# A two-layer hybrid transformer in one fp32 kernel: work from VectorE to ScalarE, and attention on two-bank PSUM tiles

## The chip, the core and the metric

The kernel runs on one core of a Trainium2 chip, in one launch. The metric is the device time in microseconds (us), the median of the runs. The engines that appear are TensorE (PE; its weight loads are PEld), VectorE (DVE), ScalarE (ACT), GpSimd (POOL) and SyncE (SP, which issues the loads of weights).

## The reference

Two layers over a sequence of 256 tokens (the latents) and a context of 256 tokens, width 1024. Each layer is a SwiGLU FFN, a mixer and another FFN, each behind an RMS norm that is scaled and shifted by a modulation, and added back through a gate. The first layer's mixer is a gated depthwise convolution, the second's is attention with 8 query heads and 2 key heads of 128. The second layer's context stream ends after it has given keys and values, and its second FFN runs on the latents alone.

```python
def _modulate(t, g, shift, scale):
    return _rms(t, g) * (1 + scale) + shift

def _swiglu(h, w13, w2):
    gte, up = jnp.split(h @ w13, 2, axis=-1)
    return (jax.nn.silu(gte) * up) @ w2

def _attend(q, k, v):
    s = jnp.einsum('bqhgd,bkhd->bhgqk', q, k).astype(jnp.float32) * (ATTN_HEAD_DIM ** -0.5)
    p = jax.nn.softmax(s, axis=-1).astype(v.dtype)
    return jnp.einsum('bhgqk,bkhd->bqhgd', p, v)
...
        mod = (jax.nn.silu(c) @ mod_w[i] + mod_b[i]).reshape(bsz, 3, 3, 1, D_MODEL)
        modc = (jax.nn.silu(c_ctx) @ mod_w[i] + mod_b[i]).reshape(3, 3, D_MODEL)
        lat = lat + 0.5 * mod[:, 0, 2] * _swiglu(_modulate(lat, norm_g[i, 0], mod[:, 0, 0], mod[:, 0, 1]), ffn_w13[i, 0], ffn_w2[i, 0])
...
        if kind == MIX_CONV:
            y = _short_conv_mixer(h, conv_w_in[j], conv_k[j], conv_w_out[j])
...
        elif kind == MIX_ATTN:
            y, yc = _gqa_mixer(h, hc, ctx_out, attn_w_qkv[j], attn_q_g[j], attn_k_g[j], attn_w_o[j], cos, sin)
...
        lat = lat + mod[:, 1, 2] * y
```

## The kernel before

Activations lie with the features on the 128 partitions and the tokens along the free axis: `x` holds 8 feature tiles (`KT`) of 512 tokens (`T2`), 256 (`S`) of the latents (stream 0) and 256 of the context (stream 1). Every fp32 operand of a product is split into a high part rounded for TensorE (`fp32r`) and the remainder: `split` gives ScalarE the copy into the high part (L98, tiles `wh`, `gh`, `pth`) and VectorE the subtraction for the low one (L99, `wl`, `gl`, `ptl`). A product is then three matmuls, high by high, high by low and low by high (`mm3`, L122 to L124). Weights come in raw tiles `wr` of 128x2048, three buffers, loaded by SyncE, and are split in halves of 1024.

**FFN.** The 22 hidden tiles of an FFN are done in thirds of 8, 7 and 7 (`THIRDS`); behind each third `project` multiplies by w2 and `finish` adds the gated result to `x` (L446, VectorE, one step for each stream). Most hidden tiles of the first three FFNs are pairs (class `Pair`): gate and up of one hidden tile are a 2x2 block product done with seven products of half depth in place of eight (a scheme of Strassen's kind, with sums of weights `S1` to `S4`, sums of activations `T1` to `T4`, and the blocks `A11`, `A12`, `A22`). There are 54 pairs. A pair has two PSUM tiles: `p` gathers A11, S2, S3 and A22 in turn, its middle results read off by ScalarE, and `q` holds A12 in its first half and S1 and S4 in its second. `head` does A11 into p, copies it to `sg` (L585) and does A12 into q; `five` does S1 and copies it to `gm` (L591); `six` does S2, copies p to `sg` (L595), does S4, adds (L597) and applies Silu (L598); `seven` does S3 and adds (L602); `four` does A22 and multiplies (L608). The loop puts `seven` and `four` of the pair before between `five` and the end of `six` of the next pair. `sums` builds the sums of weights (L557, L563, L567) in a tile `ws`. The first pair of a third has no pair before it.

**Modulation.** The modulations of both layers are products of a row with a matrix. VectorE does them, one unit of 1024 columns for one feature tile and one stream at a time (`mod_unit`, L142, multiply and sum; its elementwise output goes to `junk`). `tick` gives out these units as filling work along the kernel: each stage calls it with a number of units that are then due, and loads the next raw tile when needed.

**Norms.** `square_add` squares on ScalarE and adds up on VectorE, one addition for each stream; `rms_inv` gets the inverse root; `norm_k` and `Blocks.block` scale on VectorE and ScalarE, and `block` also makes the T sums.

**Attention.** For each of 8 heads `scores` makes, for each half of 128 queries, a score tile of one bank `psc` (512 keys), its maximum (L1042), the bias `nb` (L1044), the exponential with its sum (L1050), 1/sum `r` (L1054), and the normalized `pn` on GpSimd (L1058). `turn` transposes pn on TensorE (L1067) into `pt`, two tiles of one bank, and splits them; `mix` multiplies with the values into `pav` and splits the result. All PSUM tiles come from one pool of six banks, and a second of two small ones. The loop runs:

```python
    for hd in range(HEADS):
        if hd + 2 < HEADS:
            pns[hd + 2] = scores(hd + 2)
        pts[hd] = turn(pns.pop(hd))
        if hd:
            mix(hd - 1, pts.pop(hd - 1))
        tick(2)
```

**Last FFN.** It runs on the latents alone. Its first 4 hidden tiles use the input before its norm (`first_mm`, a 256-token product with two more columns that carry the shift; the norm is applied behind it, `first_post`), while the norm is worked out; all eight normalized blocks are made behind tile 1. The others use `mm2`, where the high and low part lie side by side in one moving tile of 512 (L1107, L1108).

The program is written as one order of work; a scheduler then places each engine's instructions, so that an engine's order may differ from the written one. Engines wait for each other on semaphores. A tile from a pool waits until the last reader of the buffer that it takes is done.

## Time and profile before

| | us |
|---|---|
| median of 3 runs | 1587.94 |
| lowest, highest | 1587.75, 1588.68 |
| the profiled execution | 1589.78 |
| span of its trace (first to last instruction) | 1588.0 |
| mean granted clock of TensorE | 0.995 |

The profiled execution takes 1.8 us more than its span, and lies 0.1% over the median. In the page's rows an engine's busy time comes with its share of the span and the number of its instructions. In a row of a group stand the line, the engine, the operation, the tiles it writes and reads, and its count; then busy time, mean ns of one, and the idle time of the engine just before, with what ended it. Matmuls are pipelined: a record of 0.28 us overlaps the next, and the step from start to start is the price of one. The wait rows give the total, the number and the longest of the waits of a line.

### The profile page before, as it was taken

The page shows a single profiled execution, that of the slowest core. Times are in us where ns is not written, and L with a number is a line of the kernel's source. Part 1 is how long each engine was busy: PE and PEld are TensorE (multiplying, and loading weights), DVE is VectorE, ACT ScalarE, POOL GpSimd, SP SyncE. Part 2 cuts the span into 40 slices and gives each one's busy share as a digit, 9 for nine tenths or more (in the row PEclk, how much of TensorE's full clock was granted, in tenths as well). Part 3 has the DMA queues.
Part 4 walks back from the last instruction along what each step waited for, and adds up shares of the span by engine and source line. Part 5 has one row for each costly group of instructions (what it writes and reads, how often), then busy time and mean ns, then how long its engine had stood idle before and what let it go on. Part 6 is the DMA issues. An engine that isn't in the chain of part 4 may idle for free.

```text
span 1588.0 us, 25040 instructions
## 1 busy us (share of the span) xinstructions
PE 1565.0 (99%) x10210; PEld 1423.9 (90%) x10210; DVE 1319.8 (83%) x2029; ACT 738.2 (46%) x1180; POOL 29.8 (2%) x20
## 2 busy tenths in 40 slices
PE   8999999999999999999999999999999999899998
PEld 6788998998888899989899899899899898888887
DVE  5778778879998879799798899898898899976654
ACT  5532452544322356335345375335255455655543
POOL 0000000000000000000000000000000005200000
PEclk9999999999999999999999999999999999999999
DMA  8545234234565412452342423443433654645552
GB/s 319 181 174 201 92 115 167 104 117 162 186 214 193 177 65 95 142 200 104 130 177 102 160 103 107 158 161 107 175 133 122 235 186 149 234 156 186 186 202 90
DMA packets 38419, 248.74 MB, mean 157 GB/s; under 512 B 5280, under 2 KB 7072, under 8 KB 11936
## 3 DMA queue, kind: packets, MB, share of 16 engines
q1 hardware_dynamic: 35712, 245.38, 43.5%
q10 hardware_dynamic: 2592, 1.76, 0.4%
q8 instruction: 80, 1.31, 0.3%
q14 instruction: 35, 0.29, 0.1%
HBM read 244.77 MB, written 1.05 MB: 155 GB/s over the span
## 4 chain that ended last, share of the span: by engine, by line
PE 93%; DVE 3%; ACT 2%; DMA 1%; issue 1%; POOL 0%; DVEq 0%; POOLq 0%; ACTq 0%
PE py L122 9%; PE py L123 9%; PE py L124 9%; PE p L124 7%; PE p L123 7%; PE p L122 7%; PE q L122 5%; PE q L123 5%; PE q L124 5%; PE py L1107 3%; PE pg L1107 2%; PE pu L1107 2%; PE pg L122 2%; PE pg L123 1%; PE pg L124 1%; PE pu L124 1%
## 5 line engine op out<-in xcount | busy, mean ns | idle before, releaser
L98 ACT ACTIVATE wh<-wr 128x1024 fp32r<-128x1024 f32 (+2 forms) x276 | 277.2, 1015 | 352.2 <-PE py L123 81.2
L99 DVE TENSOR_TENSOR wl<-wr,wh 128x1024 fp32r<-128x1024 f32 (+2 forms) x276 | 319.7, 1166 | 78.4 <-ACT wh L98 71.0
L142 DVE CUSTOM_DVE_ANT_0 junk<-wr,scbc,modb 128x1024 bf16<-128x1024 f32 x224 | 286.8, 1280 | 25.0 <-DMA wr<-in_modT 22.2
L123 PE MATMUL py<-gl,wh 128*128 128x512 f32 (+1 forms) x570 | 213.3, 374 | 0.0
L122 PE MATMUL py<-gh,wh 128*128 128x512 f32 (+1 forms) x570 | 213.3, 374 | 0.0
L124 PE MATMUL py<-gh,wl 128*128 128x512 f32 (+1 forms) x570 | 213.0, 374 | 0.0
L99 DVE TENSOR_TENSOR wl<-ws,wh 128x1024 fp32r<-128x1024 f32 x108 | 131.3, 1223 | 28.6 <-ACT wh L98 28.1
L98 ACT ACTIVATE wh<-ws 128x1024 fp32r<-128x1024 f32 x108 | 113.4, 1058 | 75.1 <-DVE ws L563 32.5
L124 PEld LDWEIGHTS py<-gh,wl 128*128 128x128 f32 x570 | 107.3, 188 | 19.1
L122 PEld LDWEIGHTS py<-gh,wh 128*128 128x128 f32 x570 | 107.4, 188 | 18.5
L123 PEld LDWEIGHTS py<-gl,wh 128*128 128x128 f32 x570 | 107.4, 188 | 18.2
L123 PE MATMUL p<-tl,wh 128*128 128x256 f32 x432 | 122.2, 283 | 0.0
L124 PE MATMUL p<-th,wl 128*128 128x256 f32 x432 | 122.2, 283 | 0.0
L122 PE MATMUL p<-th,wh 128*128 128x256 f32 x432 | 122.2, 283 | 0.0
L122 PE MATMUL q<-bh,wh 128*128 128x256 f32 x320 | 90.6, 283 | 0.0
L123 PE MATMUL q<-bl,wh 128*128 128x256 f32 x320 | 90.6, 283 | 0.0
L124 PE MATMUL q<-bh,wl 128*128 128x256 f32 x320 | 90.6, 283 | 0.0
L122 PEld LDWEIGHTS p<-th,wh 128*128 128x128 f32 x432 | 82.9, 192 | 0.3
L123 PEld LDWEIGHTS p<-tl,wh 128*128 128x128 f32 x432 | 82.9, 192 | 0.3
L124 PEld LDWEIGHTS p<-th,wl 128*128 128x128 f32 x432 | 82.9, 192 | 0.0
L446 DVE SCALAR_TENSOR_TENSOR x<-py,G,x 128x256 f32<-128x256 f32 x144 | 62.9, 477 | 6.3 <-PE py L124 6.0
L557 DVE TENSOR_TENSOR ws<-wr 128x1024 f32<-128x1024 f32 x54 | 65.7, 1218 | 0.0
(296 smaller groups left out, 4181.1 us busy)
## 6 DMA issues: line engine op xcount, KB each, us to landing
wr<-in_w SPq DMA_DIRECT2D x88, 1024.0 KB, 4.9
wr<-in_modT SPq DMA_DIRECT2D x64, 1024.0 KB, 4.8
wr<-in_w2b SPq DMA_DIRECT2D x24, 896.0 KB, 4.6
wr<-in_w2a SPq DMA_DIRECT2D x12, 1024.0 KB, 4.8
wr<-in_mod SPq DMA_DIRECT2D x8, 1024.0 KB, 6.1
wr<-in_cw_cx SPq DMA_DIRECT2D x8, 1024.0 KB, 4.8
wr<-in_w2l SPq DMA_DIRECT2D x8, 1024.0 KB, 4.8
wr<-in_cw_b SPq DMA_DIRECT2D x4, 1024.0 KB, 4.9
```

Source lines behind the costliest of these rows:

```text
L98: nc.scalar.activation(out=hi, in_=src, func=AF.Copy)
L99: nc.vector.tensor_tensor(out=lo, in0=src, in1=hi.bitcast(F32), op=ALU.subtract)
L122: nc.tensor.matmul(ps, wh, mh, start=first, stop=False, **kw)
L123: nc.tensor.matmul(ps, wh, ml, start=False, stop=False, **kw)
L124: nc.tensor.matmul(ps, wl, mh, start=False, stop=last, **kw)
L142: nc.vector.tensor_tensor_reduce(out=junk, in0=raw[:, j * D : j * D + D], in1=scbc[:, v, :], scale=1.0, scalar=modb[:, l, col : col + 1], ...
L446: nc.vector.scalar_tensor_tensor(out=x[:, m, s * S : s * S + S], in0=ps[:, o : o + S], scalar=g[:, m, s : s + 1], in1=x[:, m, s * S : s * ...
L557: tt(out=sm.rearrange("p (a b c) -> p a b c", a=2, b=2)[:, :, 0, :], in0=a21.unsqueeze(1).to_broadcast([P, 2, T2]), in1=self.raw[:, T2 : 3 ...
L1107: nc.tensor.matmul(ps, w[0], m, start=first, stop=False, skip_group_check=True)
```

## The change

- **Modulation**: where both streams are wanted, the context's unit is now done for a whole raw tile by VectorE's product over 2048 columns, in place, and two summing passes of ScalarE (`mod_both`). `tick` can tie a unit behind a given instruction. A fourth raw buffer is added, and the tile `ws` goes.
- **finish**: on 512 tokens ScalarE scales each stream by its gate into `fy`, and VectorE adds both at once.
- **Norms**: the sums of squares are one addition over 512 tokens; `block` multiplies four tiles at once on VectorE and ScalarE applies scale and shift.
- **Pairs**: A11 goes into the first half of q, ScalarE copies it from q to p, A12 is added onto it in q. S2, S3 and A22 follow on p as before. Silu of the first half is taken straight from q, and the addition of the second half is over 256 tokens. The order of the weights' blocks in memory is changed, and the sums of weights are made in the raw tile. The order of products is A11, S3 of the pair before, A12, S1, A22 of the pair before, S2, S4; each pair with one before it ticks half a unit.
- **PSUM**: six shared tiles become three of a side a and three of a side b, and attention has pools of its own: two score tiles of two banks, one transpose tile of two banks, and two tiles for values and mixes.
- **Attention**: maximum, bias, 1/sum, the low part of the split and the transposes work on both halves of queries at once. GpSimd's normalization goes; the mix is multiplied by 1/sum, which TensorE spreads over the partitions by 16 matmuls against the identity. The loop does `turn` before `scores`, and ticks no units. The exponential's table is loaded early.
- **Last FFN**: five first tiles in place of four, and the normalized blocks in two halves behind tiles 2 and 3.

In the order of TensorE's instructions the scores of the first heads also come earlier among the value projections. The diff, cut:

```diff
+FIRST = 5
...
+    use_banks(("psm", 3), ("pss", 2))
...
+    turns = [0]
+
+    def psum(s="ps", side=None):
+
+        if side is None:
+            turns[0] += 1
+            side = "ab"[turns[0] % 2]
+        return banks["psm"].tile([P, T2], F32, tag=side, name=nm(s))
...
-        raw = wp.tile([P, 2048], F32, name=nm("wr"), tag="wr", bufs=3)
+        raw = wp.tile([P, 2048], F32, name=nm("wr"), tag="wr", bufs=4)
...
+    def mod_both(l, ch, pair, raw):
+
+        mt = mod_tile(l, ch)
+        r3 = raw.rearrange("p (j d) -> p j d", j=2)
+        nc.vector.tensor_tensor(
+            out=r3, in0=r3, in1=scbc[:, 1, :].unsqueeze(1).to_broadcast([P, 2, D]), op=ALU.mult
+        )
+        for j in range(2):
+            kt = pair * 2 + j
+            part = raw[:, j * D : j * D + D]
+            nc.scalar.activation(
+                out=part, in_=part, func=AF.Identity, accum_out=mt[:, kt, 1:2]
+            )
+        done[l, ch] += 2
...
+    def tick(n, behind=None):
 
         owed[0] += n
         while (jobs or units) and owed[0] >= 1:
-            owed[0] -= 1
-            next_unit()
+            if behind is None:
+                owed[0] -= next_unit()
+            else:
+                with tc.issue_after(behind.ins):
+                    owed[0] -= next_unit()
...
+            if not fine:
+                nc.vector.tensor_tensor(
+                    out=raw.rearrange("p (k t) -> p k t", k=4),
+                    in0=x[:, 4 * hf : 4 * hf + 4, s * S : s * S + S],
+                    in1=ri.unsqueeze(1).to_broadcast([P, 4, S]), op=ALU.mult,
+                )
             for i in range(4):
                 k = 4 * hf + i
                 c = slice(i * S, i * S + S)
+                b = B[:, k, s : s + 1]
+                if not fine:
+                    nc.scalar.activation(
+                        out=raw[:, c], in_=raw[:, c], func=AF.Identity,
+                        scale=A[:, k, s : s + 1], bias=b,
+                    )
+                    continue
...
+        if c1 - c0 == T2:
+            t = tp.tile([P, T2], F32, name=nm("fy"), tag="gm", bufs=3)
+            for s in range(2):
+                c = slice(s * S, s * S + S)
+                nc.scalar.activation(
+                    out=t[:, c], in_=ps[:, c], func=AF.Identity, scale=g[:, m, s : s + 1]
+                )
+            nc.vector.tensor_tensor(out=x[:, m, :], in0=x[:, m, :], in1=t, op=ALU.add)
...
+                self.w["A22"] = [
+                    wp.tile([P, T2], F32R, name=nm(t), tag=t, bufs=2) for t in ("w4h", "w4l")
+                ]
+                split(*self.w["A22"], a22)
                 tt(
-                    out=sm.rearrange("p (a b c) -> p a b c", a=2, b=2)[:, :, 0, :],
-                    in0=a21.unsqueeze(1).to_broadcast([P, 2, T2]),
-                    in1=self.raw[:, T2 : 3 * T2].rearrange("p (a c) -> p a c", a=2),
-                    op=ALU.subtract,
+                    out=r4[:, 0::3, :], in0=a21.unsqueeze(1).to_broadcast([P, 2, T2]),
+                    in1=r4[:, 0::2, :], op=ALU.subtract,
                 )
-                tt(out=sm[:, T2:1024], in0=a11, in1=sm[:, :T2], op=ALU.subtract)
-                self.keep(("S1", "S2"), sm[:, :1024])
+                tt(out=a22, in0=a22, in1=a11, op=ALU.subtract)
+                self.keep(("S2", "S1"), self.raw[:, 1024:])
                 return
...
-        def head(self):
-            p, q = psum("p"), psum("q")
-            self.p, self.q, self.q1 = p[:, :S], q, q[:, S:]
+        def one(self):
+            p, q = psum("p", "a"), psum("q", "b")
+            self.p, self.q0, self.q1 = p[:, :S], q[:, :S], q[:, S:]
             self.u = p
             self.sg = tp.tile([P, T2], F32, name=nm("sg"), tag="sg", bufs=3)
-            self.prod(self.p, "A11", ("B", 0, 0))
-            nc.scalar.copy(self.sg[:, :S], self.p)
-            self.prod(q[:, :S], "A12", ("B", 1, 0))
-
-        def five(self):
+            self.prod(self.q0, "A11", ("B", 0, 0))
+            nc.scalar.copy(self.p, self.q0)
+
+        def two_five(self):
+            self.prod(self.q0, "A12", ("B", 1, 0), False)
             self.prod(self.q1, "S1", "T1")
             self.gm = tp.tile([P, T2], F32, name=nm("gm"), tag="gm", bufs=3)
             nc.scalar.copy(self.gm[:, S:], self.q1)
+            nc.scalar.activation(out=self.sg[:, :S], in_=self.q0, func=AF.Silu)
 
         def six(self):
             self.prod(self.p, "S2", "T2", False)
-            nc.scalar.copy(self.sg[:, S:], self.p)
+            g = self.sg[:, S:]
+            nc.scalar.copy(g, self.p)
             self.prod(self.q1, "S4", ("B", 1, 1), False)
-            nc.vector.tensor_tensor(out=self.sg, in0=self.q, in1=self.sg, op=ALU.add)
-            nc.scalar.activation(out=self.sg, in_=self.sg, func=AF.Silu)
+            nc.vector.tensor_tensor(out=g, in0=self.q1, in1=g, op=ALU.add)
+            nc.scalar.activation(out=g, in_=g, func=AF.Silu)
 
         def seven(self):
             self.prod(self.p, "S3", "T3", False)
-            nc.vector.tensor_tensor(
+            return nc.vector.tensor_tensor(
                 out=self.u[:, S:], in0=self.p, in1=self.gm[:, S:], op=ALU.add
...
                         pr = Pair(a["w13"][l, b, i0 + i], h)
                         pr.sums(0)
                         pr.sums(1)
-                        pr.head()
-                    pr.five()
+                        pr.one()
                     if prev:
-                        prev.seven()
-                    pr.six()
+                        tick(0.5, prev.seven())
+                    pr.two_five()
                     if prev:
                         gs.append(new_pair("g"))
                         prev.four(gs[-1])
+                    pr.six()
                     prev = pr
...
+    warm = ap.tile([P, 1], F32, name="warm", tag="warm", bufs=1)
+    nc.scalar.activation(out=warm, in_=scq[:, :1], func=AF.Exp, scale=0.0)
+    use_banks(("psc", 2), ("ptp", 1), ("pav", 2))
+
+    def double(pool, s):
+        return banks[pool].tile([P, 2, T2], F32, tag="t", name=nm(s))
 
     def scores(hd):
         kv = hd // (HEADS // KVH)
-        r_ = []
+        ps = double("psc", "psc")
         for qt in range(2):
             o = (hd % 2) * S + qt * P
...
+            mm3(ps[:, qt, :], tuple(t[:, o : o + P] for t in qs[hd // 2]), ks[kv], True, True)
+        sc = scq[:, 2 * hd : 2 * hd + 2]
+        mx = ap.tile([P, 2], F32, name=nm("mx"), tag="mx", bufs=3)
+        nc.vector.reduce_max(mx, ps, axis=AX.X)
+        nb = ap.tile([P, 2], F32, name=nm("nb"), tag="nb", bufs=3)
+        nc.vector.scalar_tensor_tensor(
+            out=nb, in0=mx, scalar=-1.0, in1=sc, op0=ALU.mult, op1=ALU.mult
+        )
+        e = hot("e", F32)
+        sm = ap.tile([P, 2], F32, name=nm("sm"), tag="smx", bufs=3)
+        for qt in range(2):
             nc.scalar.activation(
...
+                out=e[:, qt * T2 : qt * T2 + T2], in_=ps[:, qt, :], func=AF.Exp,
+                scale=sc[:, qt : qt + 1], bias=nb[:, qt : qt + 1],
+                accum_out=sm[:, qt : qt + 1],
+            )
+        r = ap.tile([P, 2], F32, name=nm("r"), tag="r", bufs=4)
+        nc.vector.reciprocal(r, sm)
+        return e, r
+
+    def turn(e):
+        hi, lo = hot("pth"), hot("ptl")
+        pt = double("ptp", "pt").rearrange("p a t -> p (a t)")
+        for kt in range(4):
+            for qt in range(2):
+                o = kt * S + qt * P
                 nc.tensor.transpose(
-                    pt[:, kt * P : kt * P + P], pn[qt][:, kt * P : kt * P + P], ident
+                    pt[:, o : o + P], e[:, qt * T2 + kt * P : qt * T2 + kt * P + P], ident
                 )
...
+        for c in (slice(0, T2), slice(T2, 1024)):
+            nc.scalar.activation(out=hi[:, c], in_=pt[:, c], func=AF.Copy)
+        nc.vector.tensor_tensor(out=lo, in0=pt, in1=hi.bitcast(F32), op=ALU.subtract)
+        return hi, lo
 
     aos, at = [], []
 
-    def mix(hd, pt):
+    def mix(hd, pt, r):
         kv = hd // (HEADS // KVH)
         if hd % 2 == 0:
             t = hot("a")
             at.append((t[:, :T2], t[:, T2:]))
-        po = psum("pav")
+        po = banks["pav"].tile([P, T2], F32, tag="t", name=nm("po"))
         for kt in range(4):
             vw = tuple(t[:, kv * P : kv * P + P] for t in vs[kt])
-            mm3(po[:, :S], vw, (pt[0][:, kt, :], pt[1][:, kt, :]), kt == 0, kt == 3)
+            mm3(
+                po[:, :S], vw, tuple(t[:, kt * S : kt * S + S] for t in pt), kt == 0, kt == 3
+            )
+        for qt in range(2):
+            nc.tensor.matmul(
+                po[:, S + qt * P : S + qt * P + P], r[:, qt : qt + 1].to_broadcast([P, P]),
+                ident, start=True, stop=True,
+            )
+        rb = tp.tile([P, S], F32, name=nm("rb"), tag="t", bufs=3)
+        nc.scalar.copy(rb, po[:, S:])
+        nc.vector.tensor_tensor(out=rb, in0=rb, in1=po[:, :S], op=ALU.mult)
         o = (hd % 2) * S
         ah, al = (t[:, o : o + S] for t in at[-1])
-        split(ah, al, po[:, :S])
+        split(ah, al, rb)
         aos.append((ah, al))
 
-    pns, pts = {0: scores(0)}, {}
+    es, pts = {0: scores(0)}, {}
     v_proj(2)
     v_proj(3)
-    pns[1] = scores(1)
+    es[1] = scores(1)
     for hd in range(HEADS):
+        pts[hd] = turn(es[hd][0])
         if hd + 2 < HEADS:
-            pns[hd + 2] = scores(hd + 2)
-        pts[hd] = turn(pns.pop(hd))
+            es[hd + 2] = scores(hd + 2)
         if hd:
...
+            mix(hd - 1, pts.pop(hd - 1), es.pop(hd - 1)[1])
+    mix(HEADS - 1, pts.pop(HEADS - 1), es.pop(HEADS - 1)[1])
+    use_banks(("psm", 3), ("pss", 2))
...
+    def norm_half(hf):
+        u = hot("u", F32)
+        ks = slice(4 * hf, 4 * hf + 4)
+        nc.vector.tensor_tensor(
+            out=u.rearrange("p (k t) -> p k t", k=4), in0=x[:, ks, :S],
+            in1=ris.unsqueeze(1).to_broadcast([P, 4, S]), op=ALU.mult,
+        )
+        for q in range(2):
+            t = hot("h")
+            ht.append(t)
+            for j in range(2):
+                k = 4 * hf + 2 * q + j
+                c = slice((2 * q + j) * S, (2 * q + j) * S + S)
+                kw = {"scale": A[:, k, :1], "bias": B[:, k, :1]}
+                nc.scalar.activation(
+                    out=t[:, j * T2 : j * T2 + S], in_=u[:, c], func=AF.Identity, **kw
+                )
+                nc.scalar.activation(out=u[:, c], in_=u[:, c], func=AF.Identity, **kw)
+            h4 = t.rearrange("p (j h t) -> p j h t", j=2, h=2)
+            nc.vector.tensor_tensor(
+                out=h4[:, :, 1, :],
+                in0=u[:, q * T2 : q * T2 + T2].rearrange("p (j t) -> p j t", j=2),
+                in1=h4[:, :, 0, :].bitcast(F32), op=ALU.subtract,
+            )
+
...
-        if i < 4:
+        if i < FIRST:
...
+            if i in (2, 3):
+                norm_half(i - 2)
```

More of the change, by code (lines that the diff above doesn't have):

```diff
@@ L173, in next_unit @@
             raw = load_raw(a["modT"][l, ch * 4 + pair])
[L174 to L179 removed]
+            for j in range(2):
+                units.append((1, lambda j=j: mod_unit(l, ch, pair, raw, j, 0)))
+            if streams(l, ch) == 2:
+                units.append((2, lambda: mod_both(l, ch, pair, raw)))
+        weight, unit = units.pop(0)
+        unit()
+        return weight
+    def tick(n, behind=None):
         owed[0] += n
         while (jobs or units) and owed[0] >= 1:
[L183 to L184 removed]
+            if behind is None:
[3 more added lines that the diff above has]
+                    owed[0] -= next_unit()
     def mod_ready(l, ch):
@@ L542, in __init__ @@
             self.raw = load_raw(src)
-            self.keep(("A11", "A12"), self.raw[:, 1024:])
+            self.keep(("A11", "A12"), self.raw[:, :1024])
         def keep(self, keys, part):
@@ L634, in ffn @@
                     w13_post(pp[1], gs[1], 0, T2)
-                    heads[0].head()
+                    heads[0].one()
                     h.sums(2)
@@ L703, in ffn @@
                 ws2, lambda k, c0, c1: (cur[k][0][:, c0:c1], cur[k][1][:, c0:c1]), n,
-                gate, tail if end else None, tot, 2 if end and tot == T2 else 0, ev, between,
+                gate, tail if end else None, tot, 2 if end and tot == T2 else 0, ev - 0.5 * end, between,
             )
@@ L874, in hybrid_kernel @@
         split(zs[m][0], zs[m][1], z)
-        tick(6)
+        tick(5.5)
     def by_pairs(key):
```

154 lines of the change are left out of this document (56 added, 98 removed).

## Prediction

> **What bounds the kernel now.** I read the page first: the shares of each engine and the chain that ended last.
>
> ```profile
> span 1588.0 us, 25040 instructions
> ...
> PE 1565.0 (99%) x10210; PEld 1423.9 (90%) x10210; DVE 1319.8 (83%) x2029; ACT 738.2 (46%) x1180; POOL 29.8 (2%) x20
> ...
> PE 93%; DVE 3%; ACT 2%; DMA 1%; issue 1%; POOL 0%; DVEq 0%; POOLq 0%; ACTq 0%
> ```
>
> TensorE is busy for 99% of the span. VectorE has 17% to spare, ScalarE half. So an instruction taken off VectorE is worth nothing by itself; only a TensorE wait that ends, or a matmul, counts. Next, the windows, to see where TensorE is not full and at which pitch it runs. The columns are the window, its length, busy time and count of PE, PEld, DVE, ACT and POOL, granted clock, DMA share, GB/s.
>
> ```profile
> 40.00:560.00 520.00, 519.80 (x3025) 457.23 (x3024) 440.80 (x671) 203.79 (x296) 0.00 (x0) 1.00 0.45 159
> 580.00:1320.00 740.00, 738.87 (x5232) 696.43 (x5231) 658.61 (x950) 354.47 (x539) 0.00 (x0) 1.00 0.41 143
> 170.00:200.00 30.00, 30.00 (x253) 30.00 (x252) 23.78 (x30) 16.53 (x27) 0.00 (x0) 1.00 0.20 71
> 435.00:465.00 30.00, 30.00 (x134) 24.85 (x133) 29.56 (x45) 7.75 (x9) 0.00 (x0) 1.00 0.61 215
> 1326.00:1368.00 42.00, 33.93 (x215) 28.68 (x214) 39.10 (x94) 24.66 (x58) 29.45 (x16) 0.96 0.42 152
> 1335.10:1338.50 3.40, 3.40 (x15) 3.06 (x14) 2.94 (x8) 2.33 (x6) 3.40 (x3) 0.50 0.29 39
> 1409.00:1417.00 8.00, 4.82 (x26) 4.53 (x25) 7.84 (x14) 4.27 (x11) 0.00 (x0) 0.79 0.14 38
> 1413.60:1417.00 3.40, 3.40 (x18) 3.40 (x17) 3.40 (x4) 0.34 (x1) 0.00 (x0) 0.50 0.34 89
> 570.00:578.00 8.00, 6.68 (x43) 6.31 (x42) 4.91 (x8) 4.30 (x8) 0.00 (x0) 0.79 0.17 43
> ```
>
> The two long stretches lose 0.2 and 1.1 us: the convolution, the pair loops and the projections run wall to wall. The third row is a pair loop: 253 matmuls of 256 columns in 30 us, one per 0.119 us. The fourth is a projection with 512 columns: 0.224 us each. VectorE is at 99% there and TensorE is still full. What can be won lies in attention (1326 to 1368), the last FFN (1409 to 1417) and a norm (570 to 578). The waits of TensorE between 1320 and 1420 give the reasons (in total, times, longest):
>
> ```profile
> PE pg L1107 <- ACT wh L98: 3.2, 1, 3.2
> PE pt L1067 <- POOL pn L1058: 3.0, 3, 2.0
> PE py L124 <- DVE wl L99: 1.4, 1, 1.4
> PE pt L1067 <- DVE ptl L99: 1.4, 2, 1.0
> PE pav L122 <- ACT pth L98: 1.1, 1, 1.1
> ```
>
> **Attention.** The groups between 1319 and 1368 (busy, mean ns, idle before), and a few rows of the timeline (start, duration):
>
> ```profile
> L1058 POOL TENSOR_SCALAR pn<-e,r 128x512 f32<-128x512 f32 x16 | 29.6, 1861 | 1331.8 <-DVE r L1054 1328.2 <-DVE bs L99 1.7 <-PE pt L1067 1.4
> L142 DVE CUSTOM_DVE_ANT_0 junk<-wr,scbc,modb 128x1024 bf16<-128x1024 f32 x13 | 16.6, 1275 | 0.0
> L1050 ACT ACTIVATE e<-psc,nb,scq 128x512 f32<-128x512 f32 x16 | 12.4, 777 | 10.1 <-DVE nb L1044 8.5 <-POOL pn L1058 0.9 <-DVE ptl L99 0.8
> L1042 DVE TENSOR_REDUCE mx<-psc 128x1 f32<-128x512 f32 x16 | 10.6, 682 | 0.9 <-PE psc L124 0.9
> L1067 PE MATMUL pt<-ident,pn 128*128 128x128 f32 x64 | 9.6, 281 | 4.5 <-POOL pn L1058 3.0 <-DVE ptl L99 1.4
> L123 PE MATMUL pav<-ptl,vh 128*128 128x256 f32 x32 | 9.6, 301 | 0.1
> L98 ACT ACTIVATE pth<-pt 128x512 fp32r<-128x512 f32 x16 | 9.0, 599 | 0.1
> L123 PE MATMUL psc<-kl,qh 128*128 128x512 f32 x16 | 6.5, 408 | 0.0
> L1044 DVE TENSOR_SCALAR nb<-mx,scq 128x1 f32<-128x1 f32 x16 | 2.8, 204 | 0.0
> L99 DVE TENSOR_TENSOR wl<-wr,wh 128x1024 fp32r<-128x1024 f32 x2 | 2.4, 1216 | 0.0
> ```
>
> ```profile
> 1310.85 1.95 PE L996 MATMUL kri<-ident,rq 128*128 128x128 f32 x16
> 1312.55 0.36 PE L122 MATMUL pv<-wh,hh 128*128 128x256 f32 x1
> ...
> 1334.74 0.83 PE L1067 MATMUL pt<-ident,pn 128*128 128x128 f32 x4 [1.96 <-POOL pn L1058]
> ...
> 1338.67 0.28 PE L124 MATMUL pav<-pth,vl 128*128 128x256 f32 x1
> ...
> 1338.99 0.38 ACT L98 ACTIVATE a<-pav 128x256 fp32r<-128x256 f32 x1 [1.37 <-PE pav L124]
> ```
>
> Before: of the 215 matmuls between 1326 and 1368 some 46 have 512 columns, 64 have 128 and 105 have 256. At 0.224, 0.107 (1.70 us for the 16 records from kri to the next start) and 0.119 us that is 29.7 us of the 42.0, so 12.3 us are lost: 8.1 of idle time, 1.7 from the half clock of 1335.1 to 1338.5, and the rest in matmuls that come late one by one. GpSimd's 16 normalizations, 29.6 us, pace the first heads.
>
> Added work: the division moves behind the product, and 1/sum must be spread over partitions. That is 16 fp32 matmuls of 128 columns. The 8 that make kri left 16 records, so these leave 32: 32 x 0.107 = 3.4 to 2 x 1.95 = 3.9 us; **+3.6**, all on TensorE. ScalarE's copy and VectorE's product behind each mix are beside TensorE's next head.
>
> Waits after. A maximum over 1024 columns in PSUM takes about what a 1024-column subtraction does, 1.22 us (two of 512 are 1.36). VectorE's order is maximum of head 1, maximum of head 2, then nb of head 1, and there are two score tiles, so scores of head 3 wait for both exponentials of head 1, which wait for that nb; the transposes of head 1, queued on TensorE ahead of them, wait for the same. From the end of scores 2: 0.3 + 1.22 + 0.2 + 2 x 0.78, less the matmuls' tail, about 3.2 us idle. Then the single transpose tile binds: transposes of head 1 are over only when head 0's lower half (1.22) has read it, 1.2 us. From then on TensorE has between two sets of transposes 6 x 0.224 + 12 x 0.119 + 4 x 0.107 = 3.2 us. The tile is free again after 0.3 + 2 x 0.57 (pth) + 1.22 (ptl) + 0.1 = 2.8 us, but where a maximum stands ahead of ptl in VectorE's queue (four heads) it is 0.3 + 1.34 + 0.3 + 1.22 + 1.22 = 4.3: 4 x 1.1 = 4.4 us. The last mix has only mix 6 as cover (1.8 of 2.8): 0.9. Sum 9.7, bounds 4 (no queueing) to 13.
>
> Half clock: the row of 1334.74 shows a wait of 1.96 us, and the window right behind it ran at 0.50; 3.4 us at half speed cost 1.7. A 3.2 us wait can bring this again; I count half, **0.9**. The Trainium skill, "TensorE: Matmul & The Clock Gate", section "Part 1: The HAM clock gate (the "warmup" mystery)", says that the clock halves after at least one idle window of about 3.4 us. By that neither the wait of 1.96 us nor the coming one would halve it, and the sum would be 0.9 lower; the trace disagrees with 0.50 behind a 1.96 us wait, and the trace decides.
>
> Attention: 9.7 + 0.9 - 12.3 = -1.7, with the matmuls **+1.9**.
>
> **Pairs.** The rows for the moved work: whole-program groups, and the answer for L591 alone (min/median/max ns).
>
> ```profile
> L142 DVE CUSTOM_DVE_ANT_0 junk<-wr,scbc,modb 128x1024 bf16<-128x1024 f32 x224 | 286.8, 1280 | 25.0 <-DMA wr<-in_modT 22.2
> L98 ACT ACTIVATE wh<-ws 128x1024 fp32r<-128x1024 f32 x108 | 113.4, 1058 | 75.1 <-DVE ws L563 32.5 <-PE p L123 27.8 <-PE py L123 7.4
> L446 DVE SCALAR_TENSOR_TENSOR x<-py,G,x 128x256 f32<-128x256 f32 x144 | 62.9, 477 | 6.3 <-PE py L124 6.0
> L557 DVE TENSOR_TENSOR ws<-wr 128x1024 f32<-128x1024 f32 x54 | 65.7, 1218 | 0.0
> ```
>
> ```profile
> L591 ACT COPY gm<-q x54: 352/374/377, 173.9 to 1221.1; 128x256 f32<-128x256 f32 x54
> ```
>
> A11's product now goes into q, ScalarE copies it to p, and A12's product, which adds onto q, has to wait for that copy. Before, A12 followed A11 at once. The copy is done 0.32 (1338.67 to 1338.99: a matmul's start to ScalarE's) + 0.37 + 0.05 = 0.745 us after the last A11 matmul starts. In 46 of the 54 pairs the previous pair's S3, 11 or 12 matmuls, stands between: 13 x 0.119 = 1.55, slack 0.8. That is the cover; without it each pair loses 0.625. It is missing in the first pair of a third: six have two other matmuls in between (0.745 - 3 x 0.119 = 0.39), two none (0.63): 6 x 0.39 + 2 x 0.63 = **+3.6**, bounds 3 and 6 (ScalarE busy at that moment).
>
> ScalarE's added work: 96 accumulations of 1024 columns (about 1.0 each by L98) and 144 scalings of 256 (about 0.37): some 150 us, 46% to 56% over the kernel, from 55% to some 65% in a pair loop (16.53 of 30). VectorE loses 96 units (123 us) and gets 48 products over 2048 columns, 2 x 1.22 less an overhead = 2.3, 110 us; finish loses 63 and gets 72 additions of 512 (0.69, 50 us); with norms and blocks it ends 26 to 30 us lower. All of that is beside TensorE, at nothing, since it stood full over VectorE's 99% at 435. Its price if the cover goes: in the six or seven pairs with such a unit, two accumulations (2.0 us) can stand in front of the copy; 0 to 0.8 each, **+1.5**, bounds 0 and 4. The tick tied behind S3's addition keeps VectorE's 2.3 us out of that addition's way.
>
> The fourth raw buffer lets the load queue on SyncE run one load ahead; the queue share is 0.20 to 0.61 and no TensorE wait above ends on a load: 0. Six shared PSUM tiles become three and three; a pair takes one of each, so three pairs fit as before: 0. The second scores, first scores and the early exponential's table load move under the value projections, which fill TensorE: 0 for them.
>
> **Last FFN and norms.** At 1409 TensorE waits 3.2 us for wh, because ScalarE and VectorE normalize all eight blocks at once, and gets 1.7 us of half clock behind it (1413.6). Now the blocks are spread over two tiles and a fifth tile needs none: 16 matmuls of 256 and 16 of 512 columns go, 48 of 258 come (-5.5 + 5.7 = +0.2). Each half norm still gives ScalarE eight scalings of 256 columns (0.38 each), beside the tile's two conversions (1.06 each) and about 2 us of the activations that end a tile: 7.2 us against 48 x 0.119 = 5.7 of TensorE. So two waits of 1.5 us, without half clock, take its place: 4.9 (3.2 + 1.7) to 3.0, **-1.9** (+0.2), bounds -4.9 and +1. The norm at 571 (8.0 less 6.68 idle, and a half clock) gets shorter accumulations and two-step blocks: **-0.4**, bounds -2 and +1.5. The start, where only the conversion order changes: **-0.3**, bounds +-0.5.
>
> **Sum**: 1.9 + 3.6 + 1.5 - 1.7 - 0.4 - 0.3 = **+4.6**. The profiled execution took 1589.8 us (1588.0 of span and 1.8 around it), 0.1% over the median 1587.9; the steps are the same for both, so 1594.4 for it and **1592.5** for the median. About 0.2%, 3.2 us, can be told from no change: faster is under 1584.8, slower over 1591.1.
>
> **Rivals.**
> 1. Attention runs covered: faster. If VectorE's maxima never stand ahead of ptl, its waits are 3.2 + 0.9 without half clock: 4.1 - 12.3 + 3.6 = -4.6; with the last FFN's waits hidden (-4.9 + 0.2) and no accumulation in front of a copy, 3.6 - 0.7 besides: -6.4, 1581.5. For it: pn's 29.6 us go, and the 13 units of 1.28 us in that stretch leave VectorE. Against: the written order of VectorE. It decides once two of the four heads pass. 0.20.
> 2. Gains and costs cancel: no difference. Two heads stall instead of four (-2.2), no half clock (-0.9), no unit in front of a copy (-1.5): 1587.9. 0.26.
> 3. The copy comes late in every pair: slower still. A conversion of 1.06 us that starts just ahead of the copy makes 0.32 + 1.06 + 0.37 + 0.05 = 1.80 against 1.55: 46 x 0.25 = 11.5, 1604.0. For it: ScalarE's 65% and its order. Against: ScalarE's gaps in a pair loop, one of 1.56 us in this row of the timeline. It decides once more than the slack of 0.8 us stands in front of the copy. 0.12.
>
> ```profile
> 196.84 0.63 ACT L98 ACTIVATE w4h<-wr 128x512 fp32r<-128x512 f32 x1 [1.56 <-PE p L123]
> ```
>
> 4. My forecast, 1591.1 to 1598: 0.42.
>
> The slower cases have 0.54. The range is 1582 to 1601: it takes in rival 1 down to its last 0.5 us and ends below rival 3, which leaves out about 0.1 on either side. The forecast's own is 1591.1 to 1598.
>
> **What would show it.** In the profile after: 10210 + 48 or so PE records; waits of q for the copy at eight places of 0.4 to 0.6 us and none between; transposes waiting for e (about 3 us, once) and for ptl (about 1 us, four times), one stretch at clock 0.50 or none; at the last FFN waits under 1.7 us and clock 1.00; VectorE near 1290 us, ScalarE near 890. Wrong is it if pairs with cover show waits (rival 3), or if attention takes under 50 us from 1312.8 (rival 1; it takes 55.2 to 1368 now).

## The result, and the profile after

The changed kernel takes 1615.4 us (median of 4, 1612.8 to 1616.0) against 1587.85 for the kernel before in the same comparison: 1.017 times as long, with a 95% interval of 1.0152 to 1.0187. It is slower, as forecast, but by 27.5 us and not by 4.6.

The page of the changed kernel: span, busy time by engine, and the chain that ended last.

```profile
span 1614.2 us, 25336 instructions
...
PE 1578.5 (98%) x10258; PEld 1436.5 (89%) x10258; DVE 1280.8 (79%) x1742; ACT 908.7 (56%) x1587; POOL 0.2 (0%) x4
...
PE 86%; DVE 7%; ACT 5%; issue 1%; DMA 1%; ACTq 0%; DVEq 0%
```

The counts are near those forecast: 48 more PE records, VectorE 39 us lower (26 to 30 forecast), ScalarE 170 us higher (150). The chain tells the rest: VectorE holds 7% of it (before 3%), ScalarE 5% (before 2%). Setting the start of each stage's first matmul beside that of the kernel before gives, for 26.2 us of span:

| stretch (us in the kernel before) | forecast | measured |
|---|---|---|
| start, first tiles (0 to 169) | -0.3 | -0.8 |
| the six pair loops outside the fronts | +3.8 | +6.0 |
| norm ahead of the convolution (346 to 523) | 0 | +3.8 |
| norm, front and pairs of the second FFN (523 to 654) | +0.2 | +7.4 |
| the same of the third FFN (877 to 1004) | +0.6 | +8.9 |
| norm and projections of attention (1227 to 1313) | 0 | +1.8 |
| attention (1313 to 1390) | +1.9 | +0.8 |
| last FFN and end | -1.7 | -1.8 |

(The forecast's 3.6 us of copies is set down where the first pairs stand: 0.39 in each of six loops, 0.63 at each of two fronts.) Of the 21.6 us between 4.6 and 26.2, 21.1 lie in the four rows where a norm hands over to the next product. The windows of the changed kernel for these places (length, busy of PE, PEld, DVE, ACT, POOL, clock, DMA share, GB/s):

```profile
385.00:415.00 30.00, 27.16 (x204) 26.39 (x203) 28.12 (x53) 18.42 (x37) 0.00 (x0) 0.94 0.32 105
570.00:617.00 47.00, 41.38 (x307) 39.62 (x306) 33.81 (x41) 28.57 (x47) 0.00 (x0) 0.93 0.13 45
930.00:980.00 50.00, 44.33 (x331) 42.80 (x331) 36.09 (x45) 29.91 (x50) 0.00 (x0) 0.93 0.12 43
1340.00:1396.00 56.00, 48.74 (x350) 44.42 (x349) 45.04 (x79) 35.89 (x83) 0.00 (x0) 0.97 0.38 135
607.60:614.30 6.70, 5.89 (x27) 5.89 (x28) 3.81 (x4) 3.04 (x5) 0.00 (x0) 0.50 0.29 88
```

and the like ones of the kernel before:

```profile
381.00:411.00 30.00, 29.80 (x235) 28.60 (x234) 28.56 (x62) 13.90 (x28) 0.00 (x0) 1.00 0.35 115
566.00:613.00 47.00, 45.68 (x367) 45.18 (x366) 40.00 (x55) 30.89 (x52) 0.00 (x0) 0.96 0.20 68
914.00:964.00 50.00, 49.25 (x402) 48.11 (x401) 46.99 (x68) 34.85 (x58) 0.00 (x0) 1.00 0.29 100
```

At the second FFN TensorE idles 5.6 us in place of 1.3, and yet no engine is full: VectorE and ScalarE have 13 and 18 of 47 us free. That is a chain of waits, not a load. TensorE runs at half clock behind it, from 607.6 to 614.4 us. ScalarE's and VectorE's timelines of the changed kernel show the chain:

```profile
583.83 2.08 ACT L358 ACTIVATE hr<-hr,mod,A 128x256 f32<-128x256 f32 x4 [4.93 <-DVE hr L348]
585.94 1.06 ACT L117 ACTIVATE bh<-hr 128x1024 fp32r<-128x1024 f32 x1
589.46 2.08 ACT L358 ACTIVATE hr<-hr,mod,A 128x256 f32<-128x256 f32 x4 [2.47 <-DVE hr L348]
```

```profile
582.57 1.22 DVE L348 TENSOR_TENSOR hr<-x,ss 128x1024 f32<-128x1024 f32 x1 [2.40 <-PE ss L296]
585.94 1.22 DVE L391 TENSOR_TENSOR hr<-hr,hr 128x1024 f32<-128x1024 f32 x1 [2.15 <-ACT hr L358]
587.08 1.22 DVE L118 TENSOR_TENSOR bl<-hr,bh 128x1024 fp32r<-128x1024 f32 x1
588.22 1.21 DVE L348 TENSOR_TENSOR hr<-x,ss 128x1024 f32<-128x1024 f32 x1
```

VectorE waits 2.15 us for ScalarE (585.94) with the second half's product (L348) behind it in its queue; ScalarE then waits 2.47 us for that product (589.46). Each engine waits for the other in turn.

### The profile page after: what moved, and what is told of

Read it like the earlier page. It is cut to its first block, busy times and chain, and to the rows that moved or that the text cites. A ratio compares the mean times of both kernels' runs of the same rounds, so it can differ in the third digit from the quotient of the medians.

```text
span 1614.2 us, 25336 instructions
## 1 busy us (share of the span) xinstructions
PE 1578.5 (98%) x10258; PEld 1436.5 (89%) x10258; DVE 1280.8 (79%) x1742; ACT 908.7 (56%) x1587; POOL 0.2 (0%) x4
## 3 DMA queue, kind: packets, MB, share of 16 engines
q8 instruction: 80, 1.31, 0.3%
## 4 chain that ended last, share of the span: by engine, by line
PE 86%; DVE 7%; ACT 5%; issue 1%; DMA 1%; ACTq 0%; DVEq 0%
PE py L141 8%; PE py L142 8%; PE py L143 8%; PE q L141 6%; PE q L143 6%; PE q L142 6%; PE p L143 5%; PE p L141 5%; PE p L142 5%; PE py L1187 3%; PE pg L1187 2%; PE pu L1187 2%; PE py L1188 1%; PE pg L142 1%; PE pg L141 1%; PE pu L141 1%
## 5 line engine op out<-in xcount | busy, mean ns | idle before, releaser
L118 DVE TENSOR_TENSOR wl<-wr,wh 128x1024 fp32r<-128x1024 f32 (+2 forms) x384 | 447.9, 1182 | 130.8 <-ACT wh L117 123.8
L117 ACT ACTIVATE wh<-wr 128x1024 fp32r<-128x1024 f32 (+2 forms) x384 | 390.5, 1028 | 248.7 <-PE py L142 55.8
L161 DVE CUSTOM_DVE_ANT_0 junk<-wr,scbc,modb 128x1024 bf16<-128x1024 f32 x128 | 163.9, 1281 | 21.6 <-DMA wr<-in_modT 20.5
L141 PE MATMUL q<-bh,wh 128*128 128x256 f32 x480 | 138.0, 287 | 3.7 <-ACT p L654 3.1
L193 ACT ACTIVATE wr<-wr 128x1024 f32<-128x1024 f32 x96 | 101.0, 1055 | 69.7 <-DVE wr L187 51.6
L142 PE MATMUL q<-bl,wh 128*128 128x256 f32 x480 | 136.4, 284 | 0.0
L187 DVE TENSOR_TENSOR wr<-wr,scbc 128x2048 f32<-128x2048 f32 x48 | 109.8, 2287 | 0.8
L141 PEld LDWEIGHTS q<-bh,wh 128*128 128x128 f32 x480 | 92.8, 193 | 5.9 <-ACT p L654 4.7
L143 PEld LDWEIGHTS q<-bh,wl 128*128 128x128 f32 x480 | 92.3, 193 | 1.2 <-DVE wl L118 1.2
L142 PEld LDWEIGHTS q<-bl,wh 128*128 128x128 f32 x480 | 92.8, 193 | 0.2
```

What stands on the lines that cost most here:

```text
L117: nc.scalar.activation(out=hi, in_=src, func=AF.Copy)
L118: nc.vector.tensor_tensor(out=lo, in0=src, in1=hi.bitcast(F32), op=ALU.subtract)
L141: nc.tensor.matmul(ps, wh, mh, start=first, stop=False, **kw)
L142: nc.tensor.matmul(ps, wh, ml, start=False, stop=False, **kw)
L143: nc.tensor.matmul(ps, wl, mh, start=False, stop=last, **kw)
L161: nc.vector.tensor_tensor_reduce(out=junk, in0=raw[:, j * D : j * D + D], in1=scbc[:, v, :], scale=1.0, scalar=modb[:, l, col : col + 1], ...
```

## The experiments

The runs of one kernel spread over 1 to 9 us, so that changes of 1 or 2 us are read from the stages of a trace. A trace is one execution, though, and a window of half clock more or less moves a stage by 1 or 2 us. "Theory" with a number is the name that the expectations, printed ahead of each result, give to one of the explanations. In the code, "..." stands for what is left out.

**Block as before.** In `block`, for the blocks that are not `fine`:

```diff
-            if not fine:
-                nc.vector.tensor_tensor(
...
-                    nc.scalar.activation(
-                        out=raw[:, c], in_=raw[:, c], func=AF.Identity,
-                        scale=A[:, k, s : s + 1], bias=b,
-                    )
...
+                t = scaled(s, k, A, ri)
...
                 nc.scalar.activation(out=raw[:, c], in_=t, func=AF.Identity, bias=b)
```

> The changed kernel, with block as it was before (four scalings on VectorE, one for each feature tile, in place of one product over 1024 columns and four scalings on ScalarE). Theory 1 (the two-step block starts the second and third FFN late): the losses at the fronts of these FFNs, some 17 us from 575 to 615 and from 930 to 975, go; 1597 to 1601 us. Theory 2 (the modulation units of 2048 columns hold up the norms): unchanged within 2 us, 1613 to 1616. Theory 3 (ScalarE has too much to do over the whole kernel): block gives ScalarE the same passes either way, so unchanged, 1613 to 1616.

Measured: 1604.95 us, 10.5 less. The places are those of theory 1, the size is two thirds of it: norm and front of the second FFN fall from +7.4 to +2.9, of the third from +8.9 to +2.0, and the norm of the convolution, which `block` does not touch, has 2.8 us more here, with 6.8 us of half clock (392.2 to 399.1) in place of 3.4. ScalarE's passes are as many as in the changed kernel (906 us against 909), so theory 3 doesn't hold here.

**Modulation units as before.**

```diff
-                units.append((1, lambda j=j: mod_unit(l, ch, pair, raw, j, 0)))
-            if streams(l, ch) == 2:
-                units.append((2, lambda: mod_both(l, ch, pair, raw)))
+                for v in range(streams(l, ch)):
+                    units.append((1, lambda j=j, v=v: mod_unit(l, ch, pair, raw, j, v)))
```

> The changed kernel, with every modulation unit back on VectorE as one pass of 1024 columns (no mod_both). Theory 1: only the losses ahead of the convolution and of the attention's projections go, 5 to 6 us, and some 1.5 in the pair loops: 1608 to 1610 us. Theory 2: they and the fronts of the FFNs go as well: 1595 or less. Theory 3: ScalarE loses 101 us of the 170 that were added, so some 16 of the 27 us go: 1599.

Measured: 1607.5 us, 7.9 less. The norm of the convolution goes from +3.8 to +0.3; the six pair loops outside the fronts from +6.0 to +3.7.

**Both undone.**

> Both undone in the changed kernel. Theory 1 with the part of the units: 17 and 6 us go, what is left is the copy at the first pairs (3.6), the spread of 1/sum (3.6), attention and the last FFN (-3.5) and the start (-0.8): 1591 to 1593 us. Theory 3: as with the units alone, 1599.

Measured: 1597.1 us, 18.3 less: the two gains add (10.5 + 7.9). It is 4 to 6 us over what theory 1 gave, so that a third cost is left. The waits of TensorE between 590 and 606 us of this run name it:

```profile
PE q L143 <- DVE wl L118: 1.3, 1, 1.3
PE q L141 <- ACT wh L117: 0.8, 1, 0.8
PE q L141 <- ACT p L641: 0.4, 1, 0.4
```

Weights of the first pair are late, at a place where the kernel before had no wait.

**The new block alone in the kernel before.**

> The kernel before, with the new block alone. Theory 1: slower by the 17 us of the two fronts, 1602 to 1606 us. Theories 2 and 3: within 2 us of the kernel before, 1586 to 1590.

Measured: 1596.0 us (8 runs, 1592.8 to 1602.0) against 1587.3: +8.7, interval of the ratio 1.0032 to 1.0058. The block is slower by itself, with ScalarE at its old load (740 us against 738). It gives half of the 17 us that theory 1 had put on it, and lies between the two ranges that were expected.

**Sums of weights in a tile of their own.** The kernel of the run with both undone, with

```diff
-        raw = wp.tile([P, 2048], F32, name=nm("wr"), tag="wr", bufs=4)
+        raw = wp.tile([P, 2048], F32, name=nm("wr"), tag="wr", bufs=3)
...
+                self.sm = sm = wp.tile([P, 2048], F32, name=nm("ws"), tag="ws", bufs=1)
...
```

The split of A22 also goes back behind the sums, as in the kernel before, so that three things change at once.

> The kernel of u_blockmod, with the sums of weights made in a tile of their own again (and three raw buffers, as before). Theory 4: in the raw tile the first sums of the first pair have to wait until A11's two halves are split off, since they overwrite A11; in their own tile they are ready early. Then the losses in the first pairs of the second and third FFN (3.8 and 3.0 us in u_blockmod) fall to the 0.6 of the uncovered copy each: 1591 to 1592 us. Theory 5 (it is the copy from q to p and its place in ScalarE's queue that costs there): unchanged, 1596 to 1598 us.

Measured: 1600.1 us, 3 us more and not 5 less: a miss in the total. At the place itself the waits for wh and wl are gone, as theory 4 has it, and one for the copy from q to p has taken their place (TensorE, and ScalarE's queue ahead of the copy):

```profile
600.49 0.39 PE L141 MATMUL q<-bh,wh 128*128 128x256 f32 x1 [1.57 <-ACT p L644]
```

```profile
597.65 1.05 ACT L117 ACTIVATE th<-hr 128x1024 fp32r<-128x1024 f32 x1
598.60 1.05 ACT L117 ACTIVATE wh<-ws 128x1024 fp32r<-128x1024 f32 x1
599.54 0.62 ACT L117 ACTIVATE gh<-gm 128x512 fp32r<-128x512 f32 x1
600.06 0.37 ACT L644 COPY p<-q 128x256 f32<-128x256 f32 x1
```

So both theories hold a part: the pairs of the two fronts go from 3.8 and 3.0 us to 1.6 and 1.8, and at each of them the one wait that is left, 1.6 us, is for the copy in ScalarE's queue. What was lost elsewhere (the third FFN's norm is 3.3 us longer than in the kernel before, where it was 1.2 shorter in the run with both undone, and a half-clock window follows it) was not followed further; whether the three raw buffers do that stays open.

**Finish and last FFN alone, and with attention.** The kernel before with the new `finish`, the one addition of squares and the new last FFN, and then with the new attention too:

> The kernel before, with only the new finish (gate on ScalarE, one addition on VectorE), the one addition of squares over 512 tokens, and the new last FFN. From the stages of the runs so far: last FFN -1.8, and in u_blockmod, which has this finish, the two stretches from a projection's end to the FFN behind it were 2.0 and 1.2 us shorter: 1582 to 1584 us. Theory 3 (every shift to ScalarE costs): the new finish adds 53 us to ScalarE, so slower than the last FFN alone, 1586 or more.

> The kernel of b3_finish_last with the new attention and its PSUM pools. By the prediction's sum +1.9 us against b3; by the stages of the runs so far +0.7; here nb of head 1 stands ahead of the maximum of head 2 in VectorE's order, so the wait of 3.4 us should be 2.2 us and the sum about -0.5: 1582 to 1584 us. If the two-bank tiles and the 16 matmuls are worse than the one-bank tiles at their own place, 1586 or more.

Measured: 1587.5 us (11 runs), ratio to the kernel before 0.9999 (0.9990 to 1.0008), and 1589.2 us (12 runs). In the first the last FFN gains 3.9 us, but the shorter norms that were expected did not come, so the gain that the run with both undone showed there was not finish's own. The last run below, without the new finish, has a ratio of 0.9982, 2.7 us less. That this is the price of finish, as theory 3 would have it, isn't shown: of the 3.0 us between the spans of the two traces, 2.0 lie ahead of the first projection (it starts at 125.1 and 127.1 us), where finish has not run yet. The second is 1.7 us above the first, near the 1.9 that the prediction gave attention; by the stages of the two traces attention takes 3.6 us more, with 6.8 us of half clock in the second (1336.5 to 1343.3) in place of 3.4. In this kernel nb of head 1 stands ahead of the maximum of head 2, and that did not bring the gain that was expected here: a modulation unit of 1.28 us stands between the maximum of head 1 (1331.39) and its nb (1333.72), and the wait for the exponentials is 2.7 us, not 2.2.

The difference from this kernel to the one with both undone, 1597.1 - 1589.2 = 7.9 us, is the new pair (copy, order, sums in the raw tile) with its buffers, its order of weights, the PSUM tiles in two sides and the times at which units are given out. None of these was undone alone; the sums were, together with the fourth raw buffer and the place of A22's split. By the stages 6.6 us lie in the pairs and their fronts (3.4 in the six loops, 3.2 at the two fronts); attention is 2.5 us shorter and the last FFN 3.2 us longer, for the reason given at the last run.

**Both products first.** In the changed kernel, the products of both halves are issued ahead of the first half's sums:

```diff
+                    if isinstance(h, Blocks):
+                        for part in range(2):
+                            h.mul(s, part, ri)
                     for part in range(2):
                         rest(part, ri)
```

> The changed kernel, with the products of both halves of the context's block issued on VectorE ahead of the first half's sums (in the changed kernel the second product stands behind a sum and a low half). Theory 1a (the order on VectorE starves ScalarE: 2.5 us idle at 587 to 589.5 in the changed kernel's trace): ScalarE's second set of scalings starts right behind the first half's rounding, 2.4 us earlier; at each of the two FFN fronts about 3 us less and less half clock: 1607 to 1610 us. Theory 1b (the two steps themselves, four scalings on ScalarE that can't start before a whole product of 1024 columns): unchanged within 2 us, 1613 to 1616.

Measured: 1609.15 us, 6.3 less. ScalarE's second set of scalings now starts without a wait:

```profile
585.47 2.57 ACT L368 ACTIVATE hr<-hr,mod,A 128x256 f32<-128x256 f32 x5 [4.93 <-DVE hr L346]
587.95 1.04 ACT L117 ACTIVATE bh<-hr 128x1024 fp32r<-128x1024 f32 x1
588.89 1.57 ACT L368 ACTIVATE hr<-hr,mod,A 128x256 f32<-128x256 f32 x3
```

The window 573 to 620 has 43.48 us of TensorE's 47 and a clock of 1.00. By the totals six of the 10.5 us that the block costs are an order on VectorE. By the stages the front of the second FFN gains 5.2 us, as much as by undoing the block, and that of the third only 2.5 of 6.9; whether the rest is the two steps themselves stays open.

**Two products for a modulation unit.**

```diff
-        nc.vector.tensor_tensor(out=r3, in0=r3, in1=scbc[:, 1, :]... [P, 2, D], op=ALU.mult)
         for j in range(2):
+            nc.vector.tensor_tensor(out=part, in0=part, in1=scbc[:, 1, :], op=ALU.mult)
```

> The changed kernel, with the modulation product of 2048 columns as two of 1024 columns, the summing passes on ScalarE kept. Theory 2a (a block of 2.28 us on VectorE in the norms holds them up): about half of the 7.9 us that the units cost goes, 1611 to 1612 us. Theory 2b (ScalarE's two summing passes, 1.05 us each, stand ahead of squares and roundings in its queue): unchanged or worse, 1614 to 1617.

Measured: 1607.65 us, 7.8 less: all that undoing the units gave (7.9), with ScalarE's 101 us of summing passes still there. Theory 2b falls, within this run's spread (1605.9 to 1611.1). VectorE's timeline in the changed kernel, and then in this one:

```profile
381.72 2.28 DVE L187 TENSOR_TENSOR wr<-wr,scbc 128x2048 f32<-128x2048 f32 x1
383.92 0.68 DVE L271 TENSOR_TENSOR acc<-acc,sq 128x512 f32<-128x512 f32 x1
```

```profile
381.02 1.21 DVE L190 TENSOR_TENSOR wr<-wr,scbc 128x1024 f32<-128x1024 f32 x1
382.15 0.68 DVE L269 TENSOR_TENSOR acc<-acc,sq 128x512 f32<-128x512 f32 x1
```

The addition of squares, on which the norm hangs, waits out the whole product in the one and slips in behind its half in the other.

**Both orders mended.**

> The changed kernel with both of the last two edits: both block products ahead of the sums, and modulation products of 1024 columns. All of ScalarE's added work stays. If the 18.3 us that block and units cost together come from order and size on VectorE and not from ScalarE's load, the two gains (6.3 and 7.8 us) add: 1600 to 1603 us, that is within 4 us of u_blockmod's 1597.1, with two half-clock windows less than o1_both_products. If ScalarE's load limits from here on (theory 3), they don't add: 1606 or more.

Measured: 1602.9 us, 12.5 less than the changed kernel, of 14.1 if they added in full. It is 5.8 us above the run with both undone, where under 4 was expected, and has no half-clock window less than the run with both products first (each has 17 us of it in its span). Of the 5.8 us the front of the third FFN has 4.6 (+6.4 against +1.8); whether they are ScalarE's load or the two steps of the block isn't shown.

**Matmuls in the wait.** In the attention loop of the changed kernel:

```diff
+        if hd == 0:
+            fill(banks["pav"].tile([P, T2], F32, tag="t", name=nm("idle")), 12)
```

> The changed kernel, with 12 matmuls on constants (24 records of 0.11 us, no reader) in TensorE's queue where it waits 3.4 us for the exponentials of head 1. If the idle time in one window of 3.4 us brings the half clock, the window of 0.50 in attention goes (1.7 us) and the wait shrinks to under 1 us at the same place: 1613 to 1614 us, clock 1.00 through 1350 to 1400. If the half clock has another cause, it stays.

Measured: 1615.2 us, 0.2 less, inside the spread. The same stretch in the changed kernel and in this one:

```profile
1357.00:1366.00 9.00, 4.99 (x23) 3.70 (x22) 6.47 (x11) 4.79 (x12) 0.00 (x0) 0.81 0.60 218
```

```profile
1357.00:1366.00 9.00, 7.29 (x56) 6.55 (x55) 7.66 (x13) 5.59 (x13) 0.00 (x0) 1.00 0.62 228
```

The half clock is gone from attention, which is 0.9 us shorter by the stages; 1.3 us of the wait are left, over the 1 us expected. The span of the trace is 1.3 us shorter, with one half-clock window fewer at the second FFN and one more at the third; the medians of 4 runs each can't show so little.

**The last FFN alone in the kernel before.**

> The kernel before, with the new last FFN and the one addition of squares over 512 tokens alone. The stages of the runs so far give -1.8 to -3.9 us for the last FFN: 1584 to 1587 us against 1588 of the kernel before. If ScalarE's and VectorE's work moves the wait elsewhere: 1588 or more.

Measured: 1584.7 us (11 runs), ratio 0.9982 (0.9974 to 0.9991). It beats the kernel before and the changed one. Only a part of this is what the new last FFN was made for. In its trace the stretch from 1390 us to the end is 5.0 us shorter, and some 2.9 of these come from a shorter step of TensorE in the second part of that FFN: from start to start a matmul of 512 columns takes 231 ns and not 236, so that the last projection, 352 records in each kernel, takes 61.2 us and not 62.4. The runs with finish and with attention in the kernel before have this last FFN and the short step too; the changed kernel has this last FFN with the long step, and gains 1.9 us. What sets the step stays open.

## Why the prediction was right in its sign and wrong in its size

- **The step that failed** is the line "The norm at 571 ... gets shorter accumulations and two-step blocks: -0.4, bounds -2 and +1.5", and that it was made for one place. The two-step block cost 10.5 us in the changed kernel, at two FFN fronts, and 8.7 alone in the kernel before. I counted the instructions (one product for four scalings) and not the order: a product of 1024 columns starts ScalarE at once only if it isn't itself queued behind something that waits for ScalarE. Putting the products first gave 6.3 us back; what makes up the other 4 stays open.
- **The units of 2048 columns** were priced at 0 to 0.8 us in each of six or seven pairs, as ScalarE's two passes in front of a copy: +1.5. They cost 7.9, about half in the norm ahead of the convolution, and through VectorE's 2.28 us. The term was mis-sized, and its mechanism was wrong. The two late copies in covered pairs (0.6 and 0.8 us) both belong to this term, since they are gone without the units.
- **The sums in the raw tile** were passed over as a change of layout. They overwrite A11, and so wait for its split. The new pairs cost 7.9 us by the medians and 6.6 by the stages, against the 3.6 of the sum; 3.8 of it are the copies, and the waits for late weights at the two fronts, gone with the sums in a tile of their own, are a part of the rest. No rival had it. Rival 3 put the copy's cost in the pairs with cover; there it was 0 in nearly all.
- **The copy at the first pairs** was right: TensorE waits for L654 in ten places, of which eight are the first pairs forecast; from start to start, over the pitch, these eight lose 3.8 us for 3.6. The first row is of TensorE's waits over the whole changed kernel.

```profile
PE q L141 <- ACT p L654: 3.6, 10, 0.6
PE psc L141 <- ACT e L1124: 3.6, 2, 3.4
```

- **Attention** had its waits right: the one wait for exponentials is 3.4 us for the 3.2 worked out; three waits for ptl are 2.4 us in place of four of 1.1; one half-clock window came. In all +0.8 by the stages of the changed kernel, +1.7 by the medians of the runs that add it alone and +3.6 by their stages, for +1.9; the size is known no better than that. The 32 records of the spread 1/sum are there:

```profile
L1161 PE MATMUL po<-ident,r 128*128 128x128 f32 x32 | 4.8, 273 | 0.0
```

- **The last FFN** came out at -1.8 for -1.7, and its clock at 1.00 as forecast. Its waits are 1.8 us in three, where 3.0 in two were forecast, so that the close sum is luck in part.
- **VectorE's relief** was priced at nothing, and is worth nothing: 39 us less of it, and no stage but the start (-0.8) and the last FFN is shorter. The same sentence put ScalarE's 150 us at nothing too. For the summing passes, 101 us of it, the run with two products bears that out; for the scalings of finish it is not settled. What failed is "beside TensorE": at the norms VectorE's work has no cover, and its order and the length of one instruction are what counts.

By medians that step from one kernel to the next, so that the sum is bound to come out: finish and last FFN about -0.4, attention +1.7, pairs +7.9, block +10.4, units +7.9; 27.5 in all.

## What to carry to other kernels

Where one engine is full all along, price a change at the few places where it is not: at a norm or a front VectorE's and ScalarE's instructions are on the path, and the length of a single one on a shared in-order queue counted more here than the sum of them. Before merging small instructions into a long one, or splitting a step over two engines, write down the queue order at those places and ask who waits behind whom. Undo the parts one by one: the part with a gain (here the last FFN) can be kept.

## What the runs showed of the hardware

The half clock depends on where waits fall, and not on their length alone. In the changed kernel two waits of TensorE, 1.29 and 1.31 us long, end at 606.36 and 608.41 us; the half clock sets in at 607.55, within the second, and lasts for 6.8 us:

```profile
606.36 0.38 PE L141 MATMUL q<-th,wh 128*128 128x256 f32 x1 [1.29 <-ACT wh L117]
608.41 0.58 PE L143 MATMUL q<-th,wl 128*128 128x256 f32 x1 [1.31 <-DVE wl L118]
```

The run with two products has the same pair of waits at 601 and 603 (1.46 and 1.47 us from start to start over the pitch, where the changed kernel has 1.45 and 1.48), and its clock stays at 1.00:

```profile
595.00:615.00 20.00, 15.55 (x117) 14.18 (x117) 17.39 (x21) 12.94 (x20) 0.00 (x0) 1.00 0.15 52
```

The windows at 0.50 in the changed kernel last 3.41 us or twice that, eight in its span against five in the kernel before, and start whole steps of 3.413 us apart (392.5, 607.6 and 952.3 us: 63 and 101 steps). Counted in these steps, the one ahead of 607.55 has 1.74 us of idle time; in the run with two products the two waits fall into two steps, of 1.40 and 1.21 us. How much idle time it takes isn't shown: the step ahead of the window at 1300.5 us has 0.7. The Trainium skill, "TensorE: Matmul & The Clock Gate", section "Part 1: The HAM clock gate (the "warmup" mystery)", calls the window free-running, with 3413 ns, which agrees; that it takes an idle window of about 3.4 us does not, since neither wait here was half of that.
